# Holding the late blocks of a paired projection until its last raw load has landed

## The chip, the cores and the metric

The kernel runs on 1 core of one Trainium2 chip. The metric is the device time of one execution in microseconds (us), lower is better. The profile names the core's engines: PE (matmul) with PEld (its weight loads), DVE, ACT, POOL, and SP, which here only issues DMAs. SP and POOL each put DMAs into a queue of their own.

## What is computed

One decoder layer in float32 on x of 256 x 2048: a half-step gated feed-forward net (FFN), a mixer (differential attention and an mLSTM side by side), and a second half-step FFN, each behind an RMS norm.

```python
x = x + 0.5 * swiglu(rmsnorm(x, ffn1_norm[l]), ffn1_w_gate[l], ffn1_w_up[l], ffn1_w_down[l])
h = rmsnorm(x, mix_norm[l])
a_q, a_k, a_v, m_q, m_k, m_v, m_o, m_i, m_f = jnp.split(h @ w_in[l], split_idx, axis=-1)
...
x = x + jnp.concatenate([y_a, y_b], axis=-1) @ w_out[l]
x = x + 0.5 * swiglu(rmsnorm(x, ffn2_norm[l]), ffn2_w_gate[l], ffn2_w_up[l], ffn2_w_down[l])
return rmsnorm(x, final_norm)
```

The FFN's inner width is 5632. All weights are read from HBM once (349.56 MB), and nearly all of the time goes into the projections: activations of 256 rows times weights of 2048 or 5632 rows.

## The kernel before

**Split weights.** PE multiplies a float32 product as three matmuls. Each weight tile is first cut in two: ACT writes the rounded part `wh` (line 132), DVE the rest `wl` (line 133). Lines 181 and 182 multiply by `wh`, line 184 by `wl`. Split tiles come from a pool of four (`wsp`), so the splits can run only a few tiles ahead of PE.

**Paired projections.** Two neighbouring column chunks of 512 (gate and up, or two chunks of one matrix) form one `Paired` projection, 45 in all. Its first `ns` pairs of 128-row weight blocks go through a block scheme like Winograd's form of Strassen's product, which needs fewer multiplications of blocks at the price of additions of blocks. The rest of the rows are multiplied plainly. `ns` is 5 in nearly all gate/up projections (the very first gate and up are not paired, the second has 3), 3 or 2 in the down projections, and 2 to 5 in the mixer. A projection has these stages:

- `leading` loads for each pair j a *raw* tile of three blocks: one of the first matrix, wa (line 446), and two of the second, wb, in one DMA (`load_pair`, line 208). They go through the projection's own `queue`: POOL for 40 of the 45 projections, SP for the three first gate/up projections of each FFN as far as they are paired (`ON_POOL = 3`). Raw tiles come from a pool of five (`wr`). ACT, DVE and PE work on the first block of wa, then DVE forms sums in place (line 479).
- `second_sum` uses the sums, and adds one more block in place, by a DMA that adds (line 495, POOL's queue) or on DVE (line 497).
- `sums` loads the *late* blocks, the other block of wa of each pair, two pairs to a tile (`late`, line 511, always SP's queue): three DMAs of 512, 512 and 256 KB where `ns` is 5. POOL adds each late block onto its raw tile by DMA (line 533). `bare` splits the late tile itself and multiplies it. Then come the products S3, on raw blocks that need no late block.
- `second` works through the raw tiles with the late blocks added in, and between them the plain units of wa; `third` does the last unit of wa and the plain units of wb. Plain units are loaded by `load_unit` (line 219, SP's queue).

The late tiles and the plain units share one pool of five buffers (`wrp`, tag `rawp`), so a load of line 511 or 219 waits until an older tile of that pool has been read: by its splits, and a late tile by POOL's adding DMA too.

**What sets the order.** The code only states dependences and priorities. The framework's planner makes each engine's list of instructions out of them, among those that are ready by its own estimate. On the chip an engine goes through its list in order: an instruction that waits holds everything behind it on that engine. The helper `after` (line 138) records a plain order between two instructions and no wait. The chain (`Chain.run`) lets `leading` of one projection run in turns with `third` of the one before.

Of the kernel before, what the change touches and what calls it, by code (L numbers as in the profile page):

```python
# [42 lines left out]
LK = 4  # L43
# [17 lines left out]
def tile_trunk_layer(ctx: ExitStack, tc: tile.TileContext, x, xt, par, bias_if, lamv, fnorm,  # L61
                     wg1, wu1, wd1, wqk0, wqk1, wqk2, win, wout, wg2, wu2, wd2, out):
    nc = tc.nc
# [14 lines left out]
    def nm(s):  # L78
        uid[0] += 1
        return f"{s}_{uid[0]}"  # L80
# [58 lines left out]
    def after(late, early):  # L139

        tc.add_manual_dep(late.ins, early.ins.name,
                          mybir.DependencyInfo(mybir.DependencyClass.NoSync, mybir.DependencyReason.DATA),
                          reason="order")

    def ahead_of_splits(i, ins, slack=SLACK):
        queued[i].append((len(splits) + slack, ins))

# [2 lines left out]
    def split_weights(src, hi, lo):  # L150
        made = split(src, hi, lo)
        for late, q, past in zip(made, queued, ahead):
            while q and len(splits) >= q[0][0]:
                past.append(q.pop(0)[1])
            del past[:-3]
            for early in past:
                after(late, early)
        return made
# [46 lines left out]
            f()  # L205

    def load_pair(dst, w, k, queue=nc.sync):
        queue.dma_start(dst, w[k // LK][:, k % LK:k % LK + 2, :])

    def load_unit(w, k, pieces=(UK,), spare=False):  # L210
        n = w.shape[3]
# [13 lines left out]
    def in_turn(load):  # L225
        for early in turns[-1:]:
            after(load, early)
        turns.append(load)
# [100 lines left out]
    def gained(src, gain):  # L329
        g = wk("xg")  # L330
        for i in range(2):
            ahead_of_splits(0, act.activation(g[:, i * S:(i + 1) * S], src[:, i, :], AF.Copy, scale=gain[:, i:i + 1]))
        return g.rearrange("p (a b) -> p a b", b=P)
# [16 lines left out]
    def add_part(acc, hb, c):  # L350

        t = wk("part")
        with soon():
            ahead_of_splits(0, nc.scalar.activation(t, acc, AF.Copy, scale=0.5))
        nc.gpsimd.dma_start(xres[:, hb, c * CW:(c + 1) * CW], t, accum_op=ALU.add)

    def add_half(acc, xs, scale):
        with soon():
            ahead_of_splits(1, nc.vector.scalar_tensor_tensor(xs, acc, scale, xs, op0=ALU.mult, op1=ALU.add))
# [62 lines left out]
    class Paired:  # L422
# [17 lines left out]
        def load(self, j):  # L440
            n, off = self.n, self.off
            raw = wr.tile([P, 3, n], F32, tag="raw", name=nm("raw"))
            self.raws.append(raw)
            k = self.k0 + 2 * j
            with tc.high_priority(offset=AHEAD):
                self.queue.dma_start(raw[:, 0, :], self.wa[k // LK][:, k % LK, :])
                load_pair(raw[:, 1:3, off:], self.wb, k, self.queue)
                if off:
                    nc.gpsimd.memset(raw[:, 1:3, 0:off], 0.0)

# [55 lines left out]
        def late(self, js):  # L506

            raw = wrp.tile([P, UK, self.n], F32, tag="rawp", name=nm("late"))
            k = self.k0 + 2 * js[0]
            with tc.high_priority(offset=AHEAD):  # L510
                nc.sync.dma_start(raw[:, 0:len(js), :], self.wa[k // LK][:, k % LK + 1:k % LK + 2 * len(js):2, :])
            return raw

        def bare(self, js, raw):
# [376 lines left out]
    late = {}  # L891
# [376 lines left out]
```

## Time and profile before

| what | us |
|---|---|
| median of 3 runs | 1762.99 (1758.38 to 1763.89) |
| the profiled execution | 1759.56 |
| its span in the trace | 1757.8 |
| PE busy, 7926 matmuls | 1744.6 (99%) |
| DVE busy | 1617.8 (92%) |
| ACT busy | 1267.4 (72%) |
| POOL busy | 429.3 (24%) |

A profile is one execution. The time of a program lies a little above the span of its instructions, here by 1.8 us. In the lines that follow a tile is written `out<-in`, an engine's idle time stands in brackets with what ended it, and the time to landing of a DMA runs from its issue to the signal that its data is there. Times within the span count from its start.

### The profile page before, as it was taken

Reading aid. Unit: us, or ns where it says so; the run is one execution under the profiler, and the core shown is the slowest. Engines: PE = TensorE matmul, PEld = TensorE weight load, DVE = VectorE, ACT = ScalarE, POOL = GpSimd, SP = SyncE. Lnnn points to the kernel's source line nnn. Section 1 sums busy time; section 2 is a strip of 40 time slices with the busy share of each in tenths; the row PEclk is TensorE's granted clock in tenths of the full one; section 3 lists DMA queues with packets and bytes.
Section 4 is the critical chain, followed back from the end, with each engine's and each line's share of the span. In section 5 each row is a group of like instructions: output and inputs, shape, how many; then the busy total and the mean of one; then the engine's idle time right before and its main releaser. Section 6 shows DMA issues by size and latency. Waiting matters only on the chain.

```text
span 1757.8 us, 24486 instructions
## 1 busy us (share of the span) xinstructions
PE 1744.6 (99%) x7926; PEld 1437.7 (82%) x7926; DVE 1617.8 (92%) x2189; ACT 1267.4 (72%) x1949; POOL 429.3 (24%) x630
## 2 busy tenths in 40 slices
PE   9999999999999999999999999999999999999998
PEld 7788888888888888987888888888888878888886
DVE  7999999999999999898888999999999999999997
ACT  8666777777677768777687777776777677677765
POOL 0022332322233312012231101122332332233310
PEclk9999999999999999999999999999999999999999
DMA  9787998999799977577886667898998999799973
GB/s 365 251 254 209 259 261 265 253 292 265 218 262 258 263 252 204 185 230 221 236 238 192 209 210 211 260 265 233 258 260 268 241 268 276 232 246 256 283 254 115
DMA packets 155265, 429.72 MB, mean 244 GB/s; under 512 B 17632, under 2 KB 18944, under 8 KB 154880
## 3 DMA queue, kind: packets, MB, share of 16 engines
q0 software_dynamic: 76304, 196.66, 45.1%
q1 hardware_dynamic: 77680, 229.40, 38.0%
q10 hardware_dynamic: 1152, 2.09, 0.3%
q8 instruction: 62, 1.02, 0.2%
q14 instruction: 67, 0.55, 0.1%
HBM read 349.56 MB, written 2.10 MB: 200 GB/s over the span
## 4 chain that ended last, share of the span: by engine, by line
PE 93%; DMA 2%; DVE 2%; issue 1%; ACT 0%; POOL 0%; SPq 0%; POOLq 0%; DVEq 0%; ACTq 0%
PE acc L184 18%; PE acc L181 18%; PE acc L182 18%; PE accn L181 12%; PE accn L182 12%; PE accn L184 12%; DVE wl L133 1%; DMA raw<-in_wg_dram 1%; PE tr L373 1%; DMA raw<-in_wu_dram 1%; PE tr L314 0%; PE sc L1060 0%; DMA rawp<-in_wg_dram 0%; ACT wh L132 0%; PE num L1011 0%
## 5 line engine op out<-in xcount | busy, mean ns | idle before, releaser
L132 ACT CAST wh<-raw 128x512 fp32r<-128x512 f32 (+2 forms) x885 | 601.5, 708 | 214.5 <-PE acc L182 66.3
L133 DVE TENSOR_TENSOR wl<-raw,wh 128x512 fp32r<-128x512 f32 (+2 forms) x885 | 676.1, 793 | 58.4 <-ACT wh L132 54.5
L132 ACT CAST wh<-rawp 128x1024 fp32r<-128x1024 f32 (+3 forms) x308 | 318.2, 1035 | 109.5 <-PE acc L182 55.1
L133 DVE TENSOR_TENSOR wl<-rawp,wh 128x1024 fp32r<-128x1024 f32 (+3 forms) x308 | 367.1, 1197 | 32.0 <-ACT wh L132 29.8
L181 PE MATMUL acc<-wh,xs 128*128 128x512 f32 (+2 forms) x956 | 369.5, 387 | 0.0
L182 PE MATMUL acc<-wh,xs 128*128 128x512 f32 (+2 forms) x956 | 368.9, 386 | 0.0
L184 PE MATMUL acc<-wl,xs 128*128 128x512 f32 (+2 forms) x956 | 317.6, 387 | 0.8 <-DVE wl L133 0.7
L533 POOL DMA_DIRECT2D raw<-late x176 | 152.6, 1053 | 442.7 <-DVE wl L133 422.9
L181 PE MATMUL acc<-wh,xt 128*128 128x512 f32 (+2 forms) x564 | 218.4, 388 | 0.7 <-ACT wh L132 0.7
L182 PE MATMUL acc<-wh,xt 128*128 128x512 f32 (+2 forms) x564 | 217.3, 386 | 0.0
L181 PE MATMUL accn<-wh,xt 128*128 128x512 f32 (+1 forms) x552 | 215.3, 391 | 0.0
L182 PE MATMUL accn<-wh,xt 128*128 128x512 f32 (+1 forms) x552 | 214.7, 390 | 0.0
L479 DVE TENSOR_TENSOR raw<-raw 128x1024 f32<-128x1024 f32 x176 | 211.0, 1217 | 0.8
L184 PEld LDWEIGHTS acc<-wl,xs 128*128 128x128 f32 x956 | 178.3, 188 | 39.2 <-DVE wl L133 3.6
L181 PEld LDWEIGHTS acc<-wh,xs 128*128 128x128 f32 x956 | 179.5, 188 | 36.4 <-ACT wh L132 0.6
L182 PEld LDWEIGHTS acc<-wh,xs 128*128 128x128 f32 x956 | 179.6, 188 | 35.6
L181 PE MATMUL accn<-wh,xs 128*128 128x512 f32 (+1 forms) x408 | 162.6, 400 | 1.9 <-ACT wh L132 1.9
L182 PE MATMUL accn<-wh,xs 128*128 128x512 f32 (+1 forms) x408 | 158.0, 388 | 0.0
L184 PE MATMUL acc<-wl,xt 128*128 128x512 f32 (+2 forms) x564 | 157.6, 386 | 0.0
L495 POOL DMA_DIRECT2D raw<-raw x92 | 78.9, 899 | 322.1 <-DVE wl L133 234.7
L184 PE MATMUL accn<-wl,xt 128*128 128x512 f32 (+1 forms) x552 | 154.7, 388 | 0.0
L184 PE MATMUL accn<-wl,xs 128*128 128x512 f32 (+1 forms) x408 | 140.9, 388 | 0.0
(229 smaller groups left out, 2125.0 us busy)
## 6 DMA issues: line engine op xcount, KB each, us to landing
rawp<-in_wd_dram SPq DMA_DIRECT2D x88, 512.0 KB, 5.6
raw<-late POOLq DMA_DIRECT2D x174, 256.0 KB, 5.3
raw<-in_wu_dram POOLq DMA_DIRECT2D x80, 512.0 KB, 8.4
rawp<-in_wu_dram SPq DMA_DIRECT2D x73, 512.0 KB, 5.1
rawp<-in_wg_dram SPq DMA_DIRECT2D x69, 512.0 KB, 5.2
raw<-raw POOLq DMA_DIRECT2D x92, 256.0 KB, 4.1
raw<-in_wd_dram POOLq DMA_DIRECT2D x44, 512.0 KB, 8.6
late<-in_wg_dram SPq DMA_DIRECT2D x41, 512.0 KB, 9.2
```

Of the source, the lines that this page charges most:

```text
L132: return (nc.scalar.copy(hi, src), nc.vector.tensor_tensor(out=lo, in0=src, in1=hi.bitcast(F32), op=ALU.subtract))
L133: nc.vector.tensor_tensor(out=lo, in0=src, in1=hi.bitcast(F32), op=ALU.subtract))
L181: nc.tensor.matmul(acc, lh, rh, start=first, stop=False, skip_group_check=on)
L182: nc.tensor.matmul(acc, ll, rh, start=False, stop=False, skip_group_check=on)
L184: newest[:] = [nc.tensor.matmul(acc, lh, rl, start=False, stop=last, skip_group_check=on)]
L373: nc.tensor.transpose(tr[:, i, hb * P:(hb + 1) * P], hs[hb][:, k * P:(k + 1) * P], ident)
L479: nc.vector.tensor_tensor(out=raw[:, 0:2, :], in0=raw[:, 0:3:2, :], in1=raw[:, 1:2, :].to_broadcast([P, 2, n]), op=ALU.add)
L495: nc.gpsimd.dma_start(raw[:, 0, :], raw[:, 2, :], accum_op=ALU.add)
L533: nc.gpsimd.dma_start(self.raws[j][:, 0, :], lates[-1][1][:, i, :], accum_op=ALU.add)
```

## The change

`load_pair` returns its DMA, `load` keeps the newest one, and the DMA of a late block waits until that one has landed, unless the projection's raw loads go through SP too. The new helper `landed` is like `after`, but records a real wait (`Sync` for `NoSync`). When `late` runs, all raw loads of the projection have been written down, so the newest is that of its last pair.

```diff
+    def landed(late, early):
+
+        tc.add_manual_dep(late.ins, early.ins.name,
+                          mybir.DependencyInfo(mybir.DependencyClass.Sync, mybir.DependencyReason.DATA),
+                          reason="order")
+
...
     def load_pair(dst, w, k, queue=nc.sync):
-        queue.dma_start(dst, w[k // LK][:, k % LK:k % LK + 2, :])
+        return queue.dma_start(dst, w[k // LK][:, k % LK:k % LK + 2, :])
...
                 self.queue.dma_start(raw[:, 0, :], self.wa[k // LK][:, k % LK, :])
-                load_pair(raw[:, 1:3, off:], self.wb, k, self.queue)
+                self.newest_load = load_pair(raw[:, 1:3, off:], self.wb, k, self.queue)
...
             with tc.high_priority(offset=AHEAD):
-                nc.sync.dma_start(raw[:, 0:len(js), :], self.wa[k // LK][:, k % LK + 1:k % LK + 2 * len(js):2, :])
+                load = nc.sync.dma_start(raw[:, 0:len(js), :],
+                                         self.wa[k // LK][:, k % LK + 1:k % LK + 2 * len(js):2, :])
+                if self.queue is not nc.sync:
+                    landed(load, self.newest_load)
```

The arithmetic, the sizes and the number of DMAs stay as they are.

## The prediction

> **What bounds the kernel now.** I read the page first, for the span and for the engine that is never idle.
>
> ```profile
> span 1757.8 us, 24486 instructions
> PE 1744.6 (99%) x7926; PEld 1437.7 (82%) x7926; DVE 1617.8 (92%) x2189; ACT 1267.4 (72%) x1949; POOL 429.3 (24%) x630
> ```
>
> PE is busy 99% of the span. An average can hide a starved stage, so next comes the table of busy time by stretch (columns: length, then busy time and count of PE, PEld, DVE, ACT, POOL, then granted clock, DMA share, GB/s).
>
> ```profile
> 0.00:88.00 88.00, 84.08 (x360) 66.13 (x361) 74.20 (x112) 65.48 (x100) 6.99 (x19) 1.00 0.87 308
> 88.00:700.00 612.00, 612.00 (x2749) 504.88 (x2748) 575.19 (x733) 441.23 (x654) 172.97 (x253) 1.00 0.88 251
> ...
> 1364.00:1452.00 88.00, 87.41 (x384) 70.24 (x384) 81.98 (x103) 61.81 (x91) 30.14 (x44) 1.00 0.93 262
> 1452.00:1740.00 288.00, 287.83 (x1287) 237.22 (x1286) 272.70 (x343) 205.95 (x300) 74.07 (x106) 1.00 0.85 244
> ```
>
> PE loses 3.9 us in the first 88 us, nothing from there to 700 us, 0.59 us in the fourth row and 0.17 us in the fifth. The granted clock is 1.00 in every row, so PE's time there is set by its number of matmuls: 612.00 us / 2749 = 0.223 us each. The change takes away no matmul. It can only remove PE's waits or add some.
>
> A busy mark can cover a short wait, so I also read who PE and its weight loads waited for (total us, times, longest), and keep the rows that name the split weights, since a weight load from HBM reaches PE only through them:
>
> ```profile
> PE accn L181 <- ACT wh L132: 1.9, 3, 0.9
> PE acc L181 <- ACT wh L132: 0.7, 1, 0.7
> PE acc L184 <- DVE wl L133: 0.7, 2, 0.5
> ...
> PEld acc L184 <- DVE wl L133: 4.9, 13, 1.0
> PEld accn L181 <- ACT wh L132: 3.7, 3, 1.8
> PEld acc L181 <- ACT wh L132: 1.8, 3, 1.1
> ```
>
> They make 13.7 us. Cut to the first 88 us, ahead of every projection that the change touches, the table has the rows of 1.9, 0.7 (L181) and 3.7 again whole, and this one of the sixth:
>
> ```profile
> PEld acc L181 <- ACT wh L132: 1.1, 1, 1.1
> ```
>
> So 13.7 - 1.9 - 0.7 - 3.7 - 1.1 = 6.3 us is all that any better order of weight loads could give back after that.
>
> **What is added.** Each late load (L511) of a projection whose raw loads go through POOL's queue gets one more wait on SP. The first three gate/up projections of each FFN load through SP and are left alone (the very first is not paired at all): by their numbers of paired units 2 + 3 + 3 x 3 = 14 of the 108 late loads. So 94 waits are added, in 40 of the 45 paired projections. What such a wait costs when it is met already:
>
> ```profile
> L511 SPq EVENT_SEMAPHORE  x112: 17/17/7922, 34.2 to 1701.8; - x112
> ```
>
> The median is 17 ns, 94 x 17 ns = 1.6 us on SP in all, and SP is no bound. Only the first late load of a projection can really stand; the others behind it find the wait met.
>
> **What is moved, in one projection.** I take the last gate/up pair of the first FFN: five raw pairs, three late loads (512 + 512 + 256 KB). SP's and POOL's issues in order of time, and ACT's splits of the late tiles and of the next plain units:
>
> ```profile
> 568.27 11.23 SPq L511 DMA_DIRECT2D late<-in_wg_dram  x3
> 586.12 14.00 SPq L219 DMA_DIRECT2D rawp<-in_wg_dram  x3
> ```
>
> ```profile
> 574.02 0.53 POOL L208 DMA_DIRECT2D raw<-in_wu_dram  x1
> ...
> 594.10 3.46 POOL L533 DMA_DIRECT2D raw<-late  x4 [3.93 <-DVE wl L133]
> ...
> 606.44 0.57 POOL L446 DMA_DIRECT2D raw<-in_wd_dram  x1 [6.76 <-DVE wl L133]
> ```
>
> ```profile
> 594.64 1.05 ACT L132 CAST wh<-late 128x1024 fp32r<-128x1024 f32 x1
> ...
> 597.46 0.63 ACT L132 CAST wh<-late 128x512 fp32r<-128x512 f32 x1 [0.29 <-PE acc L182]
> ...
> 602.00 1.05 ACT L132 CAST wh<-rawp 128x1024 fp32r<-128x1024 f32 x1
> ```
>
> The instructions of L208 in the window around 574.02 us hold that one load, the last raw one; its time to landing:
>
> ```profile
> DMA to landing us min/median/max: 10.7/10.7/10.7
> ```
>
> It lands at 574.0 + 10.7 = 584.7 us. The late loads now go out at 568.3 us and up to 579.5 us, in the midst of the raw loads; changed, none goes out before the landing, 16.4 us later for the first. The first reader is POOL's add at 594.10 us, then ACT's split at 594.64 us. How long the load takes there I bound by two groups of the page's DMA issues (KB, median us to landing):
>
> ```profile
> rawp<-in_wg_dram SPq DMA_DIRECT2D x69, 512.0 KB, 5.2
> late<-in_wg_dram SPq DMA_DIRECT2D x41, 512.0 KB, 9.2
> ```
>
> 9.2 us is the same load amid the raw loads, 5.2 us the same size and queue mostly outside them. The landing is then between 584.7 + 5.2 = 589.9 and 584.7 + 9.2 = 593.9 us: ahead of the first reader by 4.2 or 0.2 us. I take the shorter, because of what the DMA engines do then:
>
> ```profile
> 566.00:582.00 16.00, 16.00 (x76) 13.34 (x75) 16.00 (x21) 12.33 (x19) 4.26 (x8) 1.00 1.00 364
> 582.00:586.00 4.00, 4.00 (x20) 3.30 (x19) 4.00 (x5) 2.81 (x6) 1.61 (x2) 1.00 0.52 136
> 586.00:592.00 6.00, 6.00 (x28) 4.99 (x27) 6.00 (x11) 3.86 (x7) 1.81 (x3) 1.00 1.01 214
> 592.00:596.00 4.00, 4.00 (x19) 3.30 (x19) 3.55 (x6) 3.31 (x6) 1.90 (x3) 1.00 0.67 177
> ```
>
> They are full (share 1.00, 364 GB/s) while raw and late loads run together, and half idle from 582 to 586 us. 1280 KB of late loads are 1.31 MB / 364 GB/s = 3.6 us of that crowd; taken out, the raw loads land up to 3.6 us earlier, at 581.1 us, and the late loads fall into the hole. (If other loads take their place, the raw loads land at 584.7 us as before.) So the cover of the delay is the 9.4 us from 584.7 to 594.10 us. Gone it would be paid 1 for 1 by whatever PE cannot find to do meanwhile.
>
> Behind the late loads SP holds three plain loads of the same projection; the first went out at 586.12 us when its buffer came free, so the hold delays it by the issue of three loads, under 2 us, and its split is at 602.00 us: hidden. On POOL the adds stand in front of the next projection's raw loads, which at 606.44 us waited 6.76 us for DVE: a later add takes from that wait first.
>
> The tightest projection that I found is the last but one gate/up pair of the second FFN; its last raw load, the landing of it, and the first add:
>
> ```profile
> 1589.40 0.53 POOL L208 DMA_DIRECT2D raw<-in_wu_dram  x1 [0.15 <-issue]
> ...
> DMA to landing us min/median/max: 13.5/13.5/13.5
> ...
> 1610.40 2.58 POOL L533 DMA_DIRECT2D raw<-late  x3 [2.47 <-DVE wl L133]
> ```
>
> Landing at 1602.9 us; plus 5.2 us is 1608.1 us, 2.3 us ahead; plus 9.2 us is 1612.1 us, 1.7 us too late.
>
> Against the change speaks the rule in the Trainium skill, DMA: Bandwidth & Descriptors (Rules for kernel authors): issue a DMA early and wait for it late, so that its fixed cost is covered. By it the sum would get up to 16.4 us for each projection held like this one; by the rows above it gets 0, with 4.2 us to spare.
>
> **Sum.** Removed: the waits in which raw loads were late, of which PE shows 0.59 + 0.17 = 0.8 us in the last two stretches. Added: 0 on PE's path. Profiled time 1759.56 us (span 1757.8 us and 1.8 us around it) - 0.8 = 1758.8 us. The runs' median 1762.99 us stands 3.4 us above that execution; on it 1762.99 - 0.8 = 1762.2, so 1762 us. What a measurement here can tell from no change is about 0.3%, 5.3 us.
>
> **Rivals.**
>
> (A) *The buffers change hands, slower.* The late tiles and the plain loads share one pool of five. A load that the planner knows must wait may lose its turn on SP. That SP's order follows readiness, not the text, is seen where the next FFN's raw loads go out ahead of the output projection's late ones, which the code writes first:
>
> ```profile
> 996.86 0.33 SPq L446 DMA_DIRECT2D raw<-in_wg_dram  x1
> ...
> 1005.35 5.19 SPq L511 DMA_DIRECT2D late<-in_wout_dram  x2
> ```
>
> If three plain loads of the projection go first, they take the buffers of 568 to 579 us; two late loads get the buffers of 586.12 us and the next, the third the one that in the trace goes to the third plain load, at 586.12 + 14.00 - 0.33 = 599.8 us, after an add has been read out of it:
>
> ```profile
> SPq L219 <- DMA raw<-late: 410.7, 109, 7.9
> ```
>
> It lands 5.2 us later, at 605.0 us, 7.5 us after its split at 597.46 us. PE can first do the five S3 products, 15 x 0.223 = 3.3 us, and stands 4.2 us: in the 16 five-unit gate/up projections on POOL (8 in each FFN) 67 us, 1830 us. It decides as soon as all three plain loads go ahead; with one or two ahead, the third late load still gets a buffer that a plain unit's split frees, and this costs little. For it: five buffers, and the order seen on SP. Against: the planner can place other products into the hole. A stall of 4 us could also cost clock: the Trainium skill, TensorE: Matmul & The Clock Gate (What's actually happening) has the clock halved after an idle window of about 3.4 us. No run here shows that in mid-kernel.
>
> (B) *All waits go, faster.* If every one of the 6.3 us was crowding by late loads: 1762.99 - 6.3 = 1756.7 us, 0.36% faster. For it only that the late loads do run amid the raw ones; against it that PE shows 0.8 us of them.
>
> (C) *The late loads land slowly, slower.* After the landing they meet POOL's adds (share 1.01 from 586 to 592 us). With 9.2 us, the tight projection is 1.7 us late; 16 such cost 27 us, 1790 us; in half of them 14 us, 1777 us. It decides from 7.5 us of landing time on, the 1610.40 - 1602.9 us there.
>
> (D) *It does nothing.* Where the buffers come late anyway, or the raw loads have landed, the wait is met: 1763 us.
>
> **Chances.** The forecast 0.58, A 0.16, B 0.07, C 0.13, D 0.06. Same: the forecast, D and the smaller part of B, 0.65; faster: the rest of B, 0.06; slower: A and C, 0.29. The range goes from B, 1756 us, to C at its full price, 1790 us, and leaves A out.
>
> **What would show it.** Right: L511's first issue in each POOL projection stands at the raw landing; the median to landing of the up loads falls from that of this row, the late loads' from 9.2 towards 5.2 us; PE's table by stretch is unchanged to 1 us. Wrong by A: plain loads ahead of L511 on SP, and ACT or PE waiting for a late load. Wrong by C: POOL's add waiting for a late load. Wrong altogether if PE's order of products changes in the mixer, where I priced nothing.
>
> ```profile
> raw<-in_wu_dram POOLq DMA_DIRECT2D x80, 512.0 KB, 8.4
> ```

## The result and the profile after

| kernel | median us | runs | span of the profiled execution, us |
|---|---|---|---|
| before | 1760.68 (1758.38 to 1763.89) | 6 | 1757.8 |
| with the change | 1807.15 (1804.09 to 1813.08) | 6 | 1811.4 |

The ratio is 1.0263, 95% interval [1.0242, 1.0285]: 46.5 us slower. The forecast was no change, at most 1790 us. The traced execution with the change is the slowest of its six, 1813.08 us.

The lists of instructions are the same in both traces, entry by entry (operation, tiles and shapes), on all five engines: the planner moved nothing, and the wait is the only difference. So the 53.6 us between the two profiled spans come from when the same instructions ran. (Line numbers after line 142 move: code below it by 6, the adds of late blocks from L533 to L542.)

The page of the kernel with the change: span, busy time, and the chain that ended last (the work that the end of the span depended on, followed back step by step), by engine and by line; below it the chain of before by engine.

```profile
span 1811.4 us, 24486 instructions
...
PE 1768.7 (98%) x7926; PEld 1443.3 (80%) x7926; DVE 1619.3 (89%) x2189; ACT 1269.0 (70%) x1949; POOL 427.0 (24%) x630
...
PE 71%; DMA 12%; issue 8%; DVE 5%; POOL 2%; ACT 1%; SPq 0%; POOLq 0%; DVEq 0%; ACTq 0%
PE acc L190 13%; PE acc L187 13%; PE acc L188 13%; DMA raw<-raw 11%; PE accn L187 10%; PE accn L188 10%; PE accn L190 10%; DVE wl L133 4%; ACT wh L132 1%; PE tr L379 1%; POOL raw L501 1%; POOL raw L214 1%; POOL raw L452 0%; PE tr L320 0%; DMA raw<-in_wg_dram 0%
```

```profile
PE 93%; DMA 2%; DVE 2%; issue 1%; ACT 0%; POOL 0%; SPq 0%; POOLq 0%; DVEq 0%; ACTq 0%
```

PE's share of the chain is down from 93% to 71%, and a DMA has stepped in with 11%: `raw<-raw`, the second sum that is made by an adding DMA (L501, before L495). The DMA issues (KB, median us to landing), first of before, then of after:

```profile
raw<-raw POOLq DMA_DIRECT2D x92, 256.0 KB, 4.1
```

```profile
raw<-in_wu_dram POOLq DMA_DIRECT2D x80, 512.0 KB, 6.8
...
raw<-raw POOLq DMA_DIRECT2D x92, 256.0 KB, 8.0
...
late<-in_wg_dram SPq DMA_DIRECT2D x41, 512.0 KB, 6.3
```

The raw loads land sooner (6.8 us, 8.4 before), the late ones too once they are issued (6.3, 9.2 before), and the adds take twice as long. Who waited for the adds, before and after, and what PE waited for after (total us, times, longest):

```profile
ACT wh L132 <- DMA raw<-raw: 6.6, 14, 1.2
```

```profile
ACT wh L132 <- DMA raw<-raw: 70.5, 53, 2.7
...
PEld acc L187 <- ACT wh L132: 40.3, 32, 2.2
...
PE acc L187 <- ACT wh L132: 26.8, 25, 1.8
```

In the projection of the prediction, now at 590 to 630 us, the issues of POOL and of SP and the splits of ACT that waited:

```profile
600.13 0.53 POOL L214 DMA_DIRECT2D raw<-in_wu_dram  x1
609.64 0.87 POOL L501 DMA_DIRECT2D raw<-raw  x1 [8.98 <-DVE wl L133]
...
615.45 0.84 POOL L501 DMA_DIRECT2D raw<-raw  x1 [0.89 <-DVE xsum L350]
620.37 0.85 POOL L542 DMA_DIRECT2D raw<-late  x1 [4.08 <-DMA raw<-raw]
```

```profile
607.67 1.84 SPq L517 DMA_DIRECT2D late<-in_wg_dram  x3
```

```profile
619.99 0.62 ACT L132 CAST wh<-raw 128x512 fp32r<-128x512 f32 x1 [1.93 <-DMA raw<-raw]
621.37 0.62 ACT L132 CAST wh<-raw 128x512 fp32r<-128x512 f32 x1 [0.76 <-DMA raw<-raw]
...
623.40 0.62 ACT L132 CAST wh<-raw 128x512 fp32r<-128x512 f32 x1 [0.93 <-DMA raw<-raw]
623.92 1.04 ACT L132 CAST wh<-late 128x1024 fp32r<-128x1024 f32 x1
```

The three late loads go out in one burst at 607.67 us, when the last raw load has landed (600.13 + 7.5 us); the four adds follow from 609.64 us. The time to landing of these four, before and after:

```profile
DMA to landing us min/median/max: 3.3/4.4/5.2
```

```profile
DMA to landing us min/median/max: 7.6/7.8/8.6
```

ACT's list has the splits of the summed blocks next, so it stands for three of them, and PE behind it. The split of the late tile, at 623.92 us, waits for nothing. The table by stretch shows the two halves of the exchange (length, PE, PEld, DVE, ACT, POOL, clock, DMA share, GB/s):

```profile
592.00:608.00 16.00, 16.00 (x77) 13.30 (x76) 16.00 (x22) 13.27 (x20) 5.16 (x10) 1.00 0.81 279
608.00:612.00 4.00, 4.00 (x19) 3.34 (x18) 4.00 (x5) 1.85 (x4) 1.50 (x2) 1.00 0.63 194
612.00:616.00 4.00, 4.00 (x19) 3.30 (x19) 4.00 (x8) 1.41 (x3) 1.63 (x3) 1.00 1.02 225
616.00:620.00 4.00, 4.00 (x20) 3.30 (x19) 2.64 (x5) 1.98 (x5) 0.28 (x1) 1.00 1.09 264
620.00:624.00 4.00, 2.77 (x12) 1.77 (x10) 2.65 (x4) 2.31 (x5) 2.53 (x3) 1.00 1.06 262
```

While the raw loads run, the DMA engines are now at 0.81, not 1.00. From 612 us on they are full, and from 620 to 624 us PE is busy for 2.77 us only.

### The profile page after: what moved, and what is told of

Read it like the earlier page. It is cut to its first block, busy times and chain, and to the rows that moved or that the text cites. A ratio compares the mean times of both kernels' runs of the same rounds, so it can differ in the third digit from the quotient of the medians.

```text
span 1811.4 us, 24486 instructions
## 1 busy us (share of the span) xinstructions
PE 1768.7 (98%) x7926; PEld 1443.3 (80%) x7926; DVE 1619.3 (89%) x2189; ACT 1269.0 (70%) x1949; POOL 427.0 (24%) x630
## 4 chain that ended last, share of the span: by engine, by line
PE 71%; DMA 12%; issue 8%; DVE 5%; POOL 2%; ACT 1%; SPq 0%; POOLq 0%; DVEq 0%; ACTq 0%
PE acc L190 13%; PE acc L187 13%; PE acc L188 13%; DMA raw<-raw 11%; PE accn L187 10%; PE accn L188 10%; PE accn L190 10%; DVE wl L133 4%; ACT wh L132 1%; PE tr L379 1%; POOL raw L501 1%; POOL raw L214 1%; POOL raw L452 0%; PE tr L320 0%; DMA raw<-in_wg_dram 0%
## 5 line engine op out<-in xcount | busy, mean ns | idle before, releaser
L190 PE MATMUL acc<-wl,xs 128*128 128x512 f32 (+2 forms) x956 | 321.7, 392 | 0.4 <-DVE wl L133 0.3
L542 POOL DMA_DIRECT2D raw<-late x176 | 151.3, 963 | 515.5 <-DVE wl L133 458.0
L187 PE MATMUL accn<-wh,xs 128*128 128x512 f32 (+1 forms) x408 | 166.6, 410 | 2.1 <-ACT wh L132 2.1
L188 PE MATMUL accn<-wh,xs 128*128 128x512 f32 (+1 forms) x408 | 161.6, 397 | 0.0
L501 POOL DMA_DIRECT2D raw<-raw x92 | 78.7, 897 | 315.8 <-DVE wl L133 249.5
```

Source lines behind the costliest of these rows:

```text
L187: nc.tensor.matmul(acc, lh, rh, start=first, stop=False, skip_group_check=on)
L188: nc.tensor.matmul(acc, ll, rh, start=False, stop=False, skip_group_check=on)
L190: newest[:] = [nc.tensor.matmul(acc, lh, rl, start=False, stop=last, skip_group_check=on)]
L501: nc.gpsimd.dma_start(raw[:, 0, :], raw[:, 2, :], accum_op=ALU.add)
L542: nc.gpsimd.dma_start(self.raws[j][:, 0, :], lates[-1][1][:, i, :], accum_op=ALU.add)
```

## The experiments

The theory, *collision*: the late loads, held and let go together, meet the adding DMAs, whose results ACT reads with next to no time to spare. The rivals: *held SP queue* (the plain loads behind the held ones come late) and *late blocks late* (for their own readers). Each set of runs had the kernel before beside it, with a median of 1759.5 to 1761.9 us.

### Where the hold matters

```diff
-                if self.queue is not nc.sync:
+                if self.queue is not nc.sync and not self.by_dma:
```

The partner run has `and self.by_dma`. 92 adds are four in each of 23 projections; four of those load their raw blocks through SP, so 19 are held.

> The hold is kept only where a projection makes its second sums without adding DMAs (down, output, and the 2- and 3-pair projections). Collision (the held late loads run into the raw<-raw adding DMAs): these have none, so the kernel before, 1761 us, at most 5 us more. Held SP queue (the plain loads behind the held ones come late): these are about half of the held projections, so some 20 us slower, 1781 us. Late blocks late for their own readers: 15 to 25 us slower as well.

Measured: 1759.61 us, ratio 0.9993 [0.9983, 1.0002].

> The hold is kept only in the projections with raw<-raw adding DMAs (five pairs, POOL's queue). Collision: the whole loss, 1803 to 1808 us, and the median landing of raw<-raw at 8 us as with the change. Held SP queue or late blocks late: about half of the loss, near 1785 us.

Measured: 1809.4 us, ratio 1.0275 [1.0258, 1.0292], 1.4 us above what collision had allowed; raw<-raw took 7.6 us. The whole loss sits in the 19 held projections with adding DMAs; 21 held ones without lose nothing. Both rivals had put about half of it into each.

The trace of the change narrows it further, to 16. Three of the 19 are the mixer's, and they lie in this stretch, where PE loses nothing (it was busy 299.99 us):

```profile
700.00:1000.00 300.00, 299.99 (x1477) 252.43 (x1476) 263.99 (x437) 223.80 (x403) 64.47 (x100) 1.00 0.74 216
```

Matched one by one, the matmuls with the change run 28.1 us behind those of before at 620 us of the time of before, still 28.1 us at 1000 us, and 53.5 us at 1680 us. The time to landing of the adds, with the change, in the gate/up projections of the first FFN, in the mixer and in those of the second FFN:

```profile
DMA to landing us min/median/max: 7.1/8.8/10.9
```

```profile
DMA to landing us min/median/max: 3.3/4.1/7.1
```

```profile
DMA to landing us min/median/max: 6.1/8.2/11.1
```

In the mixer the last raw load lands 5.0 to 8.1 us before the first add, in the sixteen gate/up projections 0.2 to 3.6 us before. So the mixer has the hold and the adds, but the late loads released there are largely through when the adds go out, and its adds stay near the 3.9 us of before.

### The hold without the bytes, and with them

The late loads are as free as before. Behind the last of a projection stands one more load of the same data into the same tile, and that one is held: 8 KB in one kernel, all 1280 KB (as three loads) in another, the first tile's 512 KB in a third. The first of the three, cut at `...`:

```diff
+            for js, raw in list(zip(self.twos, loaded))[-1:]:
+                ...
+                    load = nc.sync.dma_start(raw[:, 0:1, 0:16],
+                                             self.wa[k // LK][:, k % LK + 1:k % LK + 2 * 1:2, 0:16])
+                    landed(load, self.newest_load)
```

> The late loads are free as in the kernel before; behind the last of them stands a load of 8 KB of its data once more, and that one waits for the last raw load. SP is held as long as with the change, but next to no bytes move after it. Collision: 1758 to 1768 us, raw<-raw lands in about 4 us. Held SP queue: the whole loss, 1800 us and more, with the plain loads late. Late blocks late: only the last late tile is out of reach until about 2 us after the last raw load, so no loss.

Measured: 1761.07 us, ratio 0.9998 [0.9988, 1.0007]. SP did stand: in the gate/up projections it waited at the held load (L526) for the raw landing and for the earlier late load into the same tile, which came last, 16 times. The adds kept their time:

```profile
SPq L526 <- DMA late<-in_wg_dram: 85.3, 16, 6.7
```

```profile
raw<-raw POOLq DMA_DIRECT2D x92, 256.0 KB, 4.2
```

So a queue that stands costs nothing here. It stood for less in all than with the change, where SP's waits at L517 for the up loads are 259.0 us in 18, since there the held loads come first. But the change does not send the plain loads out late either: in 14 of the 16 projections the first one goes out at the same distance from the first add as before, to 0.1 us, and the second one in all 16, because their buffers come free only then. That speaks against a held SP queue in the change itself.

> The late loads are free, and all of them are loaded a second time, into the same tiles, held until the last raw load has landed. Against the kernel that repeats only 8 KB it adds the bytes and nothing else: 1280 KB at the time of the raw<-raw adds in a five-pair projection. Collision: the whole loss again, 1800 to 1830 us, raw<-raw at 8 us. Held SP queue: the same time as the kernel that repeats 8 KB.

Measured: 1823.54 us, ratio 1.0369 [1.0339, 1.0400]. The time is as collision had it; the adds, at 6.7 us, slowed less than the 8 us expected.

> Late loads free; only the first late tile (512 KB of the 1280 KB) is loaded again once the last raw load has landed. Collision by bytes: raw<-raw at 5 to 6 us, and a part of the 63 us that the full repetition costs, 1765 to 1790 us. If any load at that time does the whole harm: 1810 us and more; if the harm needs the three of them back to back: 1761 us.

Measured: 1800.31 us, ratio 1.0217 [1.0197, 1.0238]. That is outside what collision by bytes had allowed (1765 to 1790, adds at 5 to 6 us): 40% of the bytes bring 60% of the loss. The DMA rows of the full and the partial repetition:

```profile
raw<-in_wu_dram POOLq DMA_DIRECT2D x80, 512.0 KB, 9.3
...
raw<-raw POOLq DMA_DIRECT2D x92, 256.0 KB, 6.7
```

```profile
raw<-in_wu_dram POOLq DMA_DIRECT2D x80, 512.0 KB, 8.2
...
raw<-raw POOLq DMA_DIRECT2D x92, 256.0 KB, 6.6
```

The adds suffer alike, by 2.6 and 2.5 us; what differs is the raw loads, 9.3 against 8.2 us, and no run tests whether they make up the rest of the loss.

### How long a hold it takes

```diff
-                self.newest_load = load_pair(raw[:, 1:3, off:], self.wb, k, self.queue)
+                load = load_pair(raw[:, 1:3, off:], self.wb, k, self.queue)
+                if j <= max(0, self.ns - 3):
+                    self.newest_load = load
```

The second kernel has `self.ns - 2`, the last raw load but one.

> The late loads wait for the last raw load but two (the first one where there are three pairs or less). They then go out some 4 to 5 us earlier. Collision: most of their bytes are through before the first raw<-raw add, which lands in 4 to 5 us again; 1760 to 1770 us. Held SP queue: SP is still held for most of the time, so over half of the loss stays, above 1785 us. Late blocks late: some 4 us of 16 given back, above 1790 us.

Measured: 1760.56 us, ratio 0.9998 [0.9988, 1.0007].

> The late loads wait for the last raw load but one, which lands about 2 us before the last. Collision, as a matter of how many late bytes are still under way when the adds go out: between the kernel that waits for the last but two (1761 us) and the change (1807 us), 1768 to 1790 us, raw<-raw landing in 5.5 to 7 us. If instead the waits collide only by one unlucky alignment with the very last raw load: 1761 us.

Measured: 1782.57 us, ratio 1.0119 [1.0101, 1.0138]. The rows of the two, shorter hold first:

```profile
raw<-in_wu_dram POOLq DMA_DIRECT2D x80, 512.0 KB, 7.7
...
raw<-raw POOLq DMA_DIRECT2D x92, 256.0 KB, 4.7
```

```profile
raw<-in_wu_dram POOLq DMA_DIRECT2D x80, 512.0 KB, 7.0
...
raw<-raw POOLq DMA_DIRECT2D x92, 256.0 KB, 6.6
```

### No adding DMA to run into

The second sums all go to DVE, with the hold and without it.

```diff
-                    if self.by_dma and js != self.twos[-1]:
+                    if False and js != self.twos[-1]:
```

> The change, with every second sum added on DVE in place of an adding DMA: 92 raw<-raw DMAs go, 92 DVE additions of 0.69 us come. Collision: no raw<-raw DMA is there to be run into, so this is within 8 us of its partner without the hold (free, DVE adds). Held SP queue or late blocks late: some 46 us above the partner. Both kernels may be slower than the kernel before by DVE's 63 us of more work.

Measured: 1768.6 us, ratio to before 1.0046 [1.0029, 1.0063].

> The partner: the kernel before with the second sums on DVE. No theory needs a time of its own here; up to 63 us of more DVE work, 1761 to 1824 us. It is what the kernel with hold and DVE adds is read against.

Measured: 1777.21 us, ratio to before 1.0102 [1.0075, 1.0128]. With no adding DMA the hold costs nothing; it even saves 8.6 us, a little outside the 8 us expected. The up loads land 7.1 us after issue with it, 8.8 us without. PE's weight loads waited for DVE's splits, with the hold and then without:

```profile
PEld acc L190 <- DVE wl L133: 8.2, 17, 1.3
```

```profile
PEld acc L184 <- DVE wl L133: 17.6, 27, 1.3
```

So earlier raw loads can be worth something. That they are so here because DVE has more to do (busy 1663 us in both, 1617.8 us before) is likely, but not shown.

### A longer hold

```diff
-                        nc.gpsimd.dma_start(raw[:, 0, :], raw[:, 2, :], accum_op=ALU.add)
+                        self.newest_load = nc.gpsimd.dma_start(raw[:, 0, :], raw[:, 2, :], accum_op=ALU.add)
```

> The late loads wait until the last raw<-raw add of the projection has landed, about 9 us later than with the change. Collision: raw<-raw lands in 4 to 5 us again and ACT's waits for it go back from 70 us to about 7; what is paid now is the late landing itself, ACT and POOL waiting for late tiles; the total can be above or below 1807 us. Held SP queue or late blocks late: clearly slower than with the change, 1840 us and more, as the hold is longer.

Measured: 1814.41 us, ratio 1.0297 [1.0264, 1.0330]. In this kernel a few instructions on ACT, DVE and PE also change places. The adds are quicker than ever, and now the late tiles are waited for:

```profile
raw<-raw POOLq DMA_DIRECT2D x92, 256.0 KB, 3.3
```

```profile
POOL raw L542 <- DMA late<-in_wg_dram: 123.3, 19, 8.9
ACT wh L132 <- DMA late<-in_wg_dram: 68.6, 27, 3.8
```

Of two losses of like size one has taken the other's place. The time lies below the 1840 us of the rivals, and the rows show why: late blocks can come too late for their readers, but at length they did so only with this longer hold.

### The sum by projection

Nine kernels leave DVE's work as it was. Seven of them are set out here; the hold without adds leaves the sixteen projections free, and the longer hold pays otherwise. The medians are those of the 64 adds and 80 up loads of the sixteen gate/up projections; before, they are 4.2 and 8.4 us. For each kernel, take how much longer the adds took, less how much sooner the up loads landed, and set it beside the loss over the 16 projections:

| kernel | adds, us | up loads, us | net | loss / 16, us |
|---|---|---|---|---|
| the change | 8.7 | 6.8 | 4.5 - 1.6 = 2.9 | 46.5 / 16 = 2.9 |
| hold with adds only | 8.3 | 6.8 | 4.1 - 1.6 = 2.5 | 48.7 / 16 = 3.0 |
| hold to the last but one | 7.3 | 7.0 | 3.1 - 1.4 = 1.7 | 20.7 / 16 = 1.3 |
| hold to the last but two | 5.1 | 7.7 | 0.9 - 0.7 = 0.2 | 0 |
| 8 KB again | 4.2 | 8.6 | 0.0 + 0.2 = 0.2 | 0 |
| 512 KB again | 7.3 | 8.2 | 3.1 - 0.2 = 2.9 | 38.5 / 16 = 2.4 |
| 1280 KB again | 7.5 | 9.3 | 3.3 + 0.9 = 4.2 | 64.0 / 16 = 4.0 |

The two columns agree within 0.5 us. The rule was formed after these runs, and no further run tests it; why a raw load's gain should count in full is not shown. With means in place of medians the change has 4.1 - 1.7 = 2.4 us, so the agreement of its row to the decimal is luck.

No version beat the kernel before: the best are level with it, and PE, busy 99% of the span, had little left to give.

## Why the prediction was wrong, point by point

- *PE bounds the kernel, at most 6.3 us to win.* Not contradicted: no kernel here was measurably faster. (The waits for split weights have one more row, PEld's accn L184 for DVE's wl, of 0.3 us; with it the ceiling is 6.6 us.)
- *The late loads, 16 us later, still reach their readers.* Right. Their split at 623.92 us waited for nothing, and ACT's splits and the adds of late blocks waited for late tiles at length only in the longer hold.
- *The raw loads land up to 3.6 us earlier.* Right: the last one took 7.5 us from its issue at 600.13 us, before 10.7 us.
- *What stands behind on SP and POOL is covered.* Right for SP: the plain loads go out as before. For POOL no run tests it by itself.
- *The late loads fall into the hole from 582 to 586 us; added: 0 on PE's path.* This is the step that failed. The hole was read off the DMA share alone. The work due in it, the adds of L495, goes out from 583.52 us in the trace of before:

```profile
583.52 0.87 POOL L495 DMA_DIRECT2D raw<-raw  x1 [8.97 <-DVE wl L133]
...
589.33 0.84 POOL L495 DMA_DIRECT2D raw<-raw  x1 [0.89 <-DVE xsum L344]
```

Its readers had next to no slack: ACT already waited for these adds 14 times, in the row of 6.6 us above. I asked who waits for the moved load, and not whom it would delay. In place of the 0 the adds of the sixteen gate/up projections took 4.5 us longer (8.7 against 4.2 us), and the loss was 46.5 / 16 = 2.9 us in each; by the rule above, which came after the runs, the 1.6 us that the raw loads gained make up the difference.
- *Rival C, slow landing.* It named the meeting with POOL's adds, and priced the late loads' own lateness, 27 us at most. The meeting was real; it was the other party that paid.
- *Rival A, the buffers.* The same lists of instructions rule it out. That the planner orders by readiness did not matter: on SP it kept its order.
- *The half clock.* It was named beside A for stalls of 4 us. It showed at shorter ones, below.
- *What would show it.* The late loads went out at the raw landing, and the up loads (6.8 us) and late loads (6.3 us) landed sooner, as for a right forecast; the signs of A and C did not show. Only PE's table moved, with 15.4 us lost from 88 to 700 us. None of the signs looked at the adds.

## What to carry to other kernels

When a transfer is moved, list what else uses the DMA engines at its new place and look up the reader of each: where someone already waits for a transfer briefly and often (here 14 times, 1.2 us at most), there is next to no slack, however idle the engines look. A hold does not take bytes away, it puts them beside other transfers: here the raw loads landed 1.6 us sooner and the adds of the same projections 4.5 us later. Whether that costs anything is a matter of time as much as of bytes, as the mixer and the shorter hold show. And a queue that stands is not a cost by itself: 8 KB, held until the raw loads had landed, cost nothing.

## What was not expected of the hardware

Short stalls of PE brought the half clock. PE's matmuls, and the row of the table by stretch (columns as above), with the change, around 343 us:

```profile
343.11 0.78 PE L187 MATMUL acc<-wh,xs 128*128 128x512 f32 x1 [1.63 <-ACT wh L132]
...
344.11 0.63 PE L190 MATMUL acc<-wl,xs 128*128 128x512 f32 x1
344.54 0.63 PE L187 MATMUL accn<-wh,xs 128*128 128x512 f32 x1
...
347.56 0.39 PE L190 MATMUL acc<-wl,xs 128*128 128x512 f32 x1
347.79 0.39 PE L187 MATMUL accn<-wh,xs 128*128 128x512 f32 x1
```

```profile
338.00:348.00 10.00, 7.58 (x22) 5.20 (x23) 7.44 (x10) 6.40 (x11) 4.23 (x5) 0.83 1.11 235
```

After a wait of 1.63 us the matmuls start 0.43 us apart instead of 0.23 us, for some 2.6 us, and the granted clock of those 10 us is 0.83. The trace has 8 such places, each with the granted clock at one half for 3.4 us, and about 55 slow matmuls in all; 55 x 0.20 us = 11 us of the 53.6 us between the spans. The Trainium skill, TensorE: Matmul & The Clock Gate (What's actually happening), has the clock halved after an idle window of about 3.4 us; the waits seen here were shorter, though several lay close together. In the 3.4 us ahead of the eight places PE was busy for 40 to 70% of the time, and its longest wait there was 1.8 us. In the trace of the kernel with the hold in the projections with adds alone, of an execution of 1806.14 us, there are 2 such places with about a dozen slow matmuls. So this is a part of the loss that comes and goes, not its cause.
